# Low parts of the first slabs of a stage moved from GpSimd to VectorE, and let ahead of the norm

## The chip, the cores and the metric

The kernel runs on one core of a Trainium2 chip. The metric is the device time of one execution in microseconds (us), lower is better. Engines are named as in the profile: PE is TensorE (matmuls), DVE is VectorE, ACT is ScalarE, POOL is GpSimd, SP is the engine whose queue issues the weight loads.

## The reference

Two transformer blocks on 256 tokens of width 1024, all in float32. The first block has two layers (attention, then a convolution mixer), each followed by a squared-ReLU MLP and each with a layer norm after the residual; the second block has a retention and block-attention mixer and a retrieval over 16,384 experts.

```python
for l in range(2):                                   # first block
    sh1, sc1, g1, sh2, sc2, g2 = split(silu(c) @ ada_w[l] + ada_b[l], 6)      # conditioning
    h = x * (1 + sc1) + sh1
    y = even_mixer(h, ...) if l == 0 else conv_mixer(h, ...)                  # ends in  o @ w_out
    x = layer_norm(ALPHA * x + g1 * y, ln_g[l, 0], ln_b[l, 0])
    h = x * (1 + sc2) + sh2
    x = layer_norm(ALPHA * x + g2 * (square(relu(h @ mlp_w1[l])) @ mlp_w2[l]), ln_g[l, 1], ln_b[l, 1])
h = rmsnorm(x, mix_norm_g)                           # second block
rq, rk, rv, rg, mq, mk, mv, ga, gb = split(h @ w_in)
x = x + (sigmoid(ga) * y_a + sigmoid(gb) * y_b) @ w_out
x = x + peer(rmsnorm(x, ffn_norm_g), ...)
```

## The kernel before

Tokens lie in two tiles of 128. A large product is three matmuls: an operand is split into a high part (ACT copies it into the matmul's type) and a low part (the rest, one subtraction), and `mm3` (L117 to L119) adds high x high, high x low and low x high into one accumulator. Weights come in slabs of 256 rows x 512 columns: `slab` (L121) loads one (SP, 512 KB, into one of four `raw` buffers), makes its high part `whi` (ACT, L132) and its low part `wlo` (L133). A raw buffer is free for the next load when its low part is done. `whi` and `wlo` lie in a ring of five buffers each, freed by the matmuls that read them; the last slabs of a stage use a pool of their own.

A layer norm joins two stages. There are four such places in the program, called **joins** here:

- join 1, from about 223 to 255 us: attention's output projection, then the first MLP
- join 2, 430 to 468 us: the first MLP, then the convolution mixer
- join 3, 534 to 568 us: the convolution's output projection, then the second MLP
- join 4, 736 to 775 us: the second MLP, then the second block's mixer

At a join `add_norm` runs for token tile 0 and then tile 1. Per tile: two gated sums with the residual for each half of the columns (DVE, L409 from the accumulator, then L410), the mean `ln_m` (DVE, L413), the sum of squares (ACT, L416, called the Square below), a root on ACT (L171), four tiny DVE steps (L167, L172, L173 and L175), and the normed row (DVE, L422). Then `transpose_in` transposes it on PE (L195, eight transposes of 128 x 128), scales the pieces on DVE and ACT (`full`, L209 and L204) and splits them into `hT` (ACT L140, DVE L141). Those are the operand of the next stage's first slab group, which has 48 matmuls: four slabs, tile 0's 24 matmuls and then tile 1's 24 (`skew`).

Each engine works its list in order. The lists are laid down ahead of time by a scheduler; `issue_after` tells it to put one instruction behind another. Before the change the four slabs of a first slab group are `aside`: their high parts are placed behind tile 0's Square (`self.squared`), their low parts go to POOL. All other high parts wait to be placed behind tile 1's root (`self.rooted`), with low parts on DVE. Each slab also calls `tick`, which advances the background work: the conditioning of layer 1 (`ada_sums`), whose load, ACT or DVE multiply-add (L343, L346) and small matmuls are paced by it.

Of the kernel before, what the change touches and what calls it, by code (L numbers as in the profile page):

```python
# [9 lines left out]
F32 = mybir.dt.float32  # L10
# [4 lines left out]
AF = mybir.ActivationFunctionType  # L15
OP = mybir.AluOpType
# [5 lines left out]
KD = 8  # L22
# [61 lines left out]
class Net:  # L84
    def __init__(self, tc, ins, out, dbg):
        self.tc, self.nc, self.i, self.out, self.dbg = tc, tc.nc, ins, out, dbg
        self.bg = []
        self.n, self.pace, self.credit = 0, 1.2, 0.0
        self.squared = self.rooted = None
        self.mod, self.gate = {}, {}  # L90

    def name(self, p):
# [25 lines left out]
        nc.tensor.matmul(ps, ak(a[0]), bk(b[1]), start=False, stop=False, skip_group_check=True)  # L118
        self.last = nc.tensor.matmul(ps, ak(a[1]), bk(b[0]), start=False, stop=stop, skip_group_check=True)  # L119

    def slab(self, src, k0, c0, w=512, pool=None, aside=False):  # L121

        nc = self.nc
        self.tick()
        raw = self.raw.tile([128, 2, 512], F32, name="raw")
        nc.sync.dma_start(raw[:, :, :w], src[k0 * 128:(k0 + 2) * 128, c0:c0 + w].rearrange("(k p) n -> p k n", p=128))
        pool = pool or self.wsp
        hi = pool.tile([128, 2, 512], F32R, name="whi")
        lo = pool.tile([128, 2, 512], F32R, name="wlo")
        after = self.squared if aside else self.rooted  # L130
        with self.tc.issue_after(after.ins) if after else nullcontext():
            self.high = nc.scalar.activation(hi[:, :, :w], raw[:, :, :w], AF.Copy)  # L132
        low = (nc.gpsimd if aside else nc.vector).tensor_tensor(lo[:, :, :w], raw[:, :, :w],  # L133
                                                                hi[:, :, :w].bitcast(F32), op=OP.subtract)
        if not aside:
            self.low = low
        return hi, lo

    def split(self, full, hi, lo):
# [84 lines left out]
        return g  # L224


    def lin_T(self, src, c0, n, acts, k=KD, skew=(), last=None, aside=()):


        for c in range(0, n, 512):  # L230
            w = min(512, n - c)
            slabs = {}
            for p0 in range(0, len(acts), 2):
                pair = acts[p0:p0 + 2]
                ps = [self.acc() for _ in pair]
                for k0 in range(0, k, 2):
                    if k0 not in slabs:
                        slabs[k0] = self.slab(src, k0, c0 + c, w, last if c + 512 >= n else None, c // 512 in aside)
                order = [(k0, x) for k0 in range(0, k, 2) for x in range(len(pair))]
                if c // 512 in skew:  # L240
                    order.sort(key=lambda o: o[1])
                for k0, x in order:
                    h, t = pair[x]
                    s = slice(t * 128, (t + 1) * 128)
                    for m in range(2):
                        kk = k0 + m
                        self.mm3(ps[x][:, :w], h, slabs[k0], lambda a: a[:, kk, s], lambda b: b[:, m, :w],
                                 kk == 0, kk == k - 1)
                    if k0 + 2 == k:
                        yield (h, t), c // 512, ps[x]  # L250
# [15 lines left out]
    def lin_F(self, hT, src, c0, first=False):  # L266


        if first:
            for (h, t), c, ps in self.lin_T(src, c0, 512, [(hT, 0), (hT, 1)], skew=(0,), aside=(0,)):  # L270
                o = self.wd.tile([128, 512], F32, name="mr", bufs=2)
                self.nc.scalar.activation(o, ps, AF.Copy)
                p = self.wk()
                for n in range(4):
                    self.nc.tensor.transpose(p[:, n * 128:(n + 1) * 128], o[:, n * 128:(n + 1) * 128], self.ident)
                yield slice(0, 4), slice(t * 128, (t + 1) * 128), p.rearrange("p (n t) -> p n t", n=4)
            return
        ps = [self.wk() for _ in range(2)]
        for k0 in range(0, KD, 2):
            sl = self.slab(src, k0, c0)  # L280
            for n in range(4):
                for m in range(2):
                    kk = k0 + m
                    self.mm3(ps[n // 2][:, (n % 2) * 256:(n % 2 + 1) * 256], sl, hT,
                             lambda b: b[:, m, n * 128:(n + 1) * 128], lambda a: a[:, kk, :],
                             kk == 0 and n % 2 == 0, kk == KD - 1)
        for n in range(2):
            yield slice(2 * n, 2 * n + 2), slice(0, S), ps[n].rearrange("p (n t) -> p n t", n=2)
# [113 lines left out]
    def add_norm(self, t, ps, gate):  # L402

        nc = self.nc
        r = self.wd.tile([128, D], F32, name="resid", bufs=RES)
        sm = self.sm.tile([128, 2], F32, name="ln_s")
        for c in range(2):
            s = slice(c * 512, (c + 1) * 512)
            nc.vector.tensor_tensor(r[:, s], ps[c], gate[:, s], op=OP.mult)  # L409
            nc.vector.scalar_tensor_tensor(r[:, s], self.X[:, t, s], ALPHA, r[:, s], op0=OP.mult, op1=OP.add,  # L410
                                           accum_out=sm[:, c:c + 1])
        nm = self.sm.tile([128, 1], F32, name="ln_m")
        nc.vector.scalar_tensor_tensor(nm, sm[:, 0:1], sm[:, 1:2], self.rD, op0=OP.add, op1=OP.mult)  # L413
        j = self.wd.tile([128, D], BF16, name="junk", bufs=1)
        ss = self.sm.tile([128, 1], F32, name="ln_q")
        sq = nc.scalar.activation(j, r, AF.Square, bias=nm, accum_out=ss)  # L416
        if t == 0:
            self.squared = sq
        rs = self.rsqrt_of_sum(ss)
        if t == 1:  # L420
            self.rooted = self.root
        nc.vector.tensor_scalar(r, r, nm, rs, op0=OP.add, op1=OP.mult)  # L422
        return r
# [70 lines left out]
def rope_apply(net, z, nh, cosT, sinT, dst, halfview, rstd=None):  # L494

    nc = net.nc
    n = nh * 64
    t1 = net.wa.tile([128, 512], F32, name="rp1", bufs=1)
    t2 = net.wa.tile([128, 512], F32, name="rp2", bufs=1)
    z3 = z.rearrange("p (h d) -> p h d", h=nh)  # L500
    nc.vector.tensor_tensor(t1[:, :n].rearrange("p (h d) -> p h d", h=nh), z3,
                            cosT[:, None, :].to_broadcast([128, nh, 64]), op=OP.mult)
    a, w = halfview
    zv = z.rearrange("p (h a u w) -> p h a u w", h=nh, a=a, u=2)
    tv = t2[:, :n].rearrange("p (h a u w) -> p h a u w", h=nh, a=a, u=2)
    sv = sinT.rearrange("p (a u w) -> p a u w", a=a, u=2)
    for u in range(2):
        sb = sv[:, None, :, u, :].to_broadcast([128, nh, a, w])
        if a == 1:
            nc.vector.tensor_tensor(tv[:, :, 0, u, :], zv[:, :, 0, 1 - u, :], sb[:, :, 0, :], op=OP.mult)  # L510
        else:
            nc.vector.tensor_tensor(tv[:, :, :, u, :], zv[:, :, :, 1 - u, :], sb, op=OP.mult)
    if rstd is None:
        nc.vector.tensor_tensor(dst, t1[:, :n], t2[:, :n], op=OP.add)
    else:
        nc.vector.tensor_tensor(t1[:, :n], t1[:, :n], t2[:, :n], op=OP.add)
        nc.vector.tensor_tensor(dst.rearrange("p (h d) -> p h d", h=nh), t1[:, :n].rearrange("p (h d) -> p h d", h=nh),
                                rstd[:, :, None].to_broadcast([128, nh, 64]), op=OP.mult)
# [320 lines left out]
def second_mixer(net, hT, rs, done, ahead):  # L839
    nc, tc, i = net.nc, net.tc, net.i  # L840
    w = i["w_in_2"][0]
    act = [(hT, 0), (hT, 1)]
    with tc.tile_pool(name="m2", bufs=1, reuse_waits="tile") as mp:
# [3 lines left out]
        rv = net.x8([128, NT, D])  # L847
        gq = net.bcast(i["moba_q_gain_2"], 0, 64, "mgq", mp, 1)
        gk = net.bcast(i["moba_k_gain_2"], 0, 64, "mgk", mp, 1)
        nc.gpsimd.tensor_scalar(gq, gq, 0.125, 0.0, op0=OP.mult, op1=OP.add)  # L850
        for a in range(2):
            for (h, t), c, ps in net.lin_T(w, 512 * a, 512, act, skew=(0,) if a == 0 else (), aside=(0,) if a == 0 else ()):
                o = mp.tile([128, 512], F32, name="qk_o", bufs=2)
                dr = net.sm.tile([128, 8], F32, name="dr")
                nc.vector.tensor_scalar(dr, net.decay[:, t, a, :], rs[:, t:t + 1], None, op0=OP.mult)
                rope_apply(net, ps, 8, net.tabs[:, t, 2, :], net.tabs[:, t, 3, :], o, (1, 32), dr)
                trans4(net, o, qk[:, a, :, t * 128:(t + 1) * 128])
# [711 lines left out]
```

## Time and profile before

| | |
|---|---|
| time, median of 3 runs | 1904.43 us (1893.85 to 1904.66) |
| the profiled execution, its own time | 1892.69 us |
| its span in the profile | 1890.6 us |
| PE busy | 1804.4 us, 95% of the span |
| DVE busy | 1309.6 us, 69% |
| ACT busy | 864.3 us, 46% |
| POOL busy | 258.3 us, 14% |
| mean granted TensorE clock | 0.982 |
| chain of waits that ended last, by engine | PE 80%, DVE 14%, ACT 2%, DMA 2% |

The profile is one execution. Starts are counted from the start of the span, so a table of what one engine did in a stretch can be laid beside that of another. "Idle before" is what an engine waited just ahead of an instruction, with the instruction that ended it. Most of the program is limited by PE; the question for a change off PE is where PE stands still.

### The profile page before, as it was taken

What the parts mean: (1) busy time and instruction counts of PE and PEld (TensorE: products, weight loads), DVE (VectorE), ACT (ScalarE), POOL (GpSimd) and SP (SyncE); (2) the same over time, 40 slices, a digit from 0 to 9 for tenths busy, and PEclk for the clock granted to TensorE, in tenths of its full rate; (3) what the DMA queues carried; (4) which work ended last, traced back from release to release, by engine and by line L of the source; (5) the groups of instructions that cost most, each with busy time, mean ns of one, the idle gap of its engine ahead of it and who ended that gap; (6) DMA issues with size and microseconds to landing.
All of it is one profiled execution on the core that took longest, in us unless ns stands there. A gap on an engine that the chain in (4) does not pass through costs nothing.

```text
span 1890.6 us, 28661 instructions
## 1 busy us (share of the span) xinstructions
PE 1804.4 (95%) x10676; PEld 1513.8 (80%) x10676; DVE 1309.6 (69%) x3203; ACT 864.3 (46%) x1272; POOL 258.3 (14%) x182
## 2 busy tenths in 40 slices
PE   7999989997989997999999999999999999999998
PEld 4665679895978996775876499999999988888887
DVE  3665687768777555886576889979998145555554
ACT  2444555444445542545543244454444444444443
POOL 2000110002020002000000000045655810000000
PEclk9999999998999999898999999999999999999999
DMA  9755269886747564443666156644444666666664
GB/s 357 239 200 167 68 219 314 301 277 210 252 153 231 185 189 118 153 131 93 190 199 224 45 163 185 189 124 128 129 124 123 190 206 188 188 188 188 189 189 145
DMA packets 132155, 347.36 MB, mean 184 GB/s; under 512 B 12469, under 2 KB 13517, under 8 KB 130864
## 3 DMA queue, kind: packets, MB, share of 16 engines
q1 hardware_dynamic: 126752, 331.93, 55.0%
q0 software_dynamic: 4688, 12.03, 1.9%
q8 instruction: 84, 1.38, 0.3%
q10 hardware_dynamic: 576, 1.57, 0.2%
q14 instruction: 55, 0.45, 0.1%
HBM read 343.36 MB, written 3.70 MB: 184 GB/s over the span
## 4 chain that ended last, share of the span: by engine, by line
PE 80%; DVE 14%; DMA 2%; ACT 2%; issue 1%; SPq 0%; ACTq 0%; DVEq 0%
PE acc L117 19%; PE acc L119 19%; PE acc L118 19%; PE wk L117 4%; PE wk L118 4%; PE wk L119 4%; PE wk L1161 2%; DVE ulo L1187 2%; DVE x L1151 2%; PE wk L541 2%; PE acc L1023 1%; DVE ej L1111 1%; DVE x L1152 1%; DVE W L1174 1%; PE wk L375 1%
## 5 line engine op out<-in xcount | busy, mean ns | idle before, releaser
L1186 ACT ACTIVATE uhi<-raw 128x1024 fp32r<-128x1024 f32 x256 | 271.6, 1061 | 292.4 <-PE acc L119 177.8
L133 DVE TENSOR_TENSOR wlo<-raw,whi 128x1024 fp32r<-128x1024 f32 (+1 forms) x244 | 293.3, 1213 | 146.7 <-ACT whi L132 145.1
L132 ACT ACTIVATE whi<-raw 128x1024 fp32r<-128x1024 f32 (+1 forms) x260 | 270.5, 1051 | 258.6 <-PE acc L119 83.8
L1187 DVE TENSOR_TENSOR ulo<-raw,uhi 128x1024 fp32r<-128x1024 f32 x182 | 222.6, 1223 | 174.6 <-ACT uhi L1186 174.0
L117 PE MATMUL acc<-x,uhi 128*128 128x256 f32 x1024 | 293.8, 287 | 0.0
L118 PE MATMUL acc<-X,uhi 128*128 128x256 f32 x1024 | 288.6, 282 | 0.0
L119 PE MATMUL acc<-x,ulo 128*128 128x256 f32 x1024 | 288.4, 282 | 0.0
L117 PE MATMUL acc<-whi,hT 128*128 128x512 f32 (+1 forms) x528 | 212.8, 404 | 14.3 <-ACT hT L140 12.8
L1187 POOL TENSOR_TENSOR ulo<-raw,uhi 128x1024 fp32r<-128x1024 f32 x74 | 176.9, 2392 | 353.0 <-DVE x L1152 252.1
L118 PE MATMUL acc<-wlo,hT 128*128 128x512 f32 (+1 forms) x528 | 209.2, 396 | 1.0 <-DVE wlo L133 1.0
L119 PE MATMUL acc<-whi,hT 128*128 128x512 f32 (+1 forms) x528 | 208.4, 395 | 1.1 <-DVE hT L141 1.1
L117 PE MATMUL acc<-uhi,x 128*128 128x512 f32 x512 | 202.3, 395 | 1.0 <-ACT x L140 1.0
L119 PE MATMUL acc<-uhi,x 128*128 128x512 f32 x512 | 202.3, 395 | 0.0
L118 PE MATMUL acc<-ulo,x 128*128 128x512 f32 x512 | 202.2, 395 | 0.0
L117 PEld LDWEIGHTS acc<-x,uhi 128*128 128x128 f32 x1024 | 194.2, 190 | 0.2 <-issue 0.2
L118 PEld LDWEIGHTS acc<-X,uhi 128*128 128x128 f32 x1024 | 194.1, 190 | 0.2 <-issue 0.2
L119 PEld LDWEIGHTS acc<-x,ulo 128*128 128x128 f32 x1024 | 193.9, 189 | 0.0
L117 PE MATMUL wk<-hT,whi 128*128 128x256 f32 x608 | 172.6, 284 | 0.0
L118 PE MATMUL wk<-hT,whi 128*128 128x256 f32 x608 | 172.0, 283 | 0.0
L119 PE MATMUL wk<-hT,wlo 128*128 128x256 f32 x608 | 172.0, 283 | 0.0
L117 PEld LDWEIGHTS acc<-whi,hT 128*128 128x128 f32 x528 | 101.9, 193 | 47.0 <-ACT hT L140 15.9
L119 PEld LDWEIGHTS acc<-whi,hT 128*128 128x128 f32 x528 | 101.6, 192 | 27.4 <-issue 3.9
(359 smaller groups left out, 3145.8 us busy)
## 6 DMA issues: line engine op xcount, KB each, us to landing
raw<-in_mlp_w SPq DMA_DIRECT2D x128, 512.0 KB, 5.0
raw<-in_k_ut SPq DMA_DIRECT2D x128, 512.0 KB, 3.6
raw<-in_peer_v SPq DMA_DIRECT2D x128, 512.0 KB, 3.6
adaw<-in_ada_w SPq DMA_DIRECT2D x80, 512.0 KB, 4.9
raw<-in_w_in SPq DMA_DIRECT2D x52, 512.0 KB, 3.7
raw<-in_conv_w_in SPq DMA_DIRECT2D x24, 512.0 KB, 4.7
a<-in_k_a SPq DMA_DIRECT2D x8, 1024.0 KB, 9.3
raw<-in_attn_w_in SPq DMA_DIRECT2D x16, 512.0 KB, 8.6
```

The source lines that it names most:

```text
L117: nc.tensor.matmul(ps, ak(a[0]), bk(b[0]), start=start, stop=False, skip_group_check=True)
L118: nc.tensor.matmul(ps, ak(a[0]), bk(b[1]), start=False, stop=False, skip_group_check=True)
L119: self.last = nc.tensor.matmul(ps, ak(a[1]), bk(b[0]), start=False, stop=stop, skip_group_check=True)
L132: self.high = nc.scalar.activation(hi[:, :, :w], raw[:, :, :w], AF.Copy)
L133: low = (nc.gpsimd if aside else nc.vector).tensor_tensor(lo[:, :, :w], raw[:, :, :w], hi[:, :, :w].bitcast(F32), op=OP.subtract)
L375: nc.tensor.matmul(ps[32 * j:32 * j + 32, :], self.cT[:, k, :], raw[n - 1][:, m * 512:(m + 1) * 512], start=(k == 0), stop=(k == KD - 1), ...
L541: nc.tensor.transpose(p[:, k * 128:(k + 1) * 128], src[:, k * 128:(k + 1) * 128], net.ident)
L1023: nc.tensor.matmul(ps, self.hT[:, k, t * 128:(t + 1) * 128], self.slabs[c][k // 2][:, k % 2, j * n * 128:(j + 1) * n * 128], start=(k == 0 ...
L1151: nc.vector.tensor_scalar(a, self.places, col[:, 0, m:m + 1], col[:, 2, m:m + 1], op0=OP.is_equal, op1=OP.mult)
L1161: self.net.nc.tensor.matmul(self.p[:, k * 128:(k + 1) * 128], b, a, start=True, stop=True)
L1186: nc.scalar.activation(hi, raw, AF.Copy)
L1187: (nc.gpsimd if aside else nc.vector).tensor_tensor(lo, raw, hi.bitcast(F32), op=OP.subtract)
```

## The change

`aside` becomes `early`. The first slab group's low parts go to DVE like all the others; its high parts are no longer tied to tile 0's Square, nor to anything else, so the scheduler may put high and low parts ahead of the norm; and these slabs no longer call `tick`, so 4 background steps' worth of pace are left out at each of the four joins. Low parts on DVE are noted in `self.low` in every case, which the conditioning follows. A scale of a 64-wide vector (L850) goes from POOL to DVE with it.

```diff
-    def slab(self, src, k0, c0, w=512, pool=None, aside=False):
+    def slab(self, src, k0, c0, w=512, pool=None, early=False):
         nc = self.nc
-        self.tick()
+        if not early:
+            self.tick()
...
-        after = self.squared if aside else self.rooted
+        after = None if early else self.rooted
         with self.tc.issue_after(after.ins) if after else nullcontext():
             self.high = nc.scalar.activation(hi[:, :, :w], raw[:, :, :w], AF.Copy)
-        low = (nc.gpsimd if aside else nc.vector).tensor_tensor(lo[:, :, :w], raw[:, :, :w],
-                                                                hi[:, :, :w].bitcast(F32), op=OP.subtract)
-        if not aside:
-            self.low = low
+        self.low = nc.vector.tensor_tensor(lo[:, :, :w], raw[:, :, :w], hi[:, :, :w].bitcast(F32), op=OP.subtract)
...
-        sq = nc.scalar.activation(j, r, AF.Square, bias=nm, accum_out=ss)
-        if t == 0:
-            self.squared = sq
+        nc.scalar.activation(j, r, AF.Square, bias=nm, accum_out=ss)
...
-        nc.gpsimd.tensor_scalar(gq, gq, 0.125, 0.0, op0=OP.mult, op1=OP.add)
+        nc.vector.tensor_scalar(gq, gq, 0.125, None, op0=OP.mult)
```

How the lists move, at join 4. First DVE, from the last low parts of the second MLP to tile 0's normed row (the changed file's lines are two to four lower: L133 is L134 there, L409 L407, L422 L418). Before:

```order
L133 TENSOR_TENSOR wlo<-raw,whi 128x1024 x4
L409 TENSOR_TENSOR resid<-acc,gate 128x512
L410 SCALAR_TENSOR_TENSOR resid,ln_s<-X,resid 128x512
L409 TENSOR_TENSOR resid<-acc,gate 128x512
L410 SCALAR_TENSOR_TENSOR resid,ln_s<-X,resid 128x512
L413 SCALAR_TENSOR_TENSOR ln_m<-ln_s,rD 128x1
```

and of the change:

```order
L134 TENSOR_TENSOR wlo<-raw,whi 128x1024 x6
L407 TENSOR_TENSOR resid<-acc,gate 128x512
L134 TENSOR_TENSOR wlo<-raw,whi 128x1024
L408 SCALAR_TENSOR_TENSOR resid,ln_s<-X,resid 128x512
L407 TENSOR_TENSOR resid<-acc,gate 128x512
L134 TENSOR_TENSOR wlo<-raw,whi 128x1024
L408 SCALAR_TENSOR_TENSOR resid,ln_s<-X,resid 128x512
L407 TENSOR_TENSOR resid<-acc,gate 128x512
L411 SCALAR_TENSOR_TENSOR ln_m<-ln_s,rD 128x1
```

All four low parts of the first slab group now stand ahead of tile 0's mean. At joins 1 to 3 they are spread in the same way, at joins 1 and 2 all four ahead of the Square's result, at join 3 the last just ahead of the normed row.

Second, ACT at join 4, from the second MLP's last slabs to the root. Before:

```order
L132 ACTIVATE whi<-raw 128x1024 x4
L416 ACTIVATE junk,ln_q<-resid,ln_m 128x1024
L132 ACTIVATE whi<-raw 128x1024
L171 ACTIVATE rv_q<-ln_q,eps 128x1
L132 ACTIVATE whi<-raw 128x1024 x3
```

and of the change:

```order
L133 ACTIVATE whi<-raw 128x1024 x8
L414 ACTIVATE junk,ln_q<-resid,ln_m 128x1024
L169 ACTIVATE rv_q<-ln_q,eps 128x1
L414 ACTIVATE junk,ln_q<-resid,ln_m 128x1024
L202 ACTIVATE full<-wk,af3B,af3A 128x128 x2
```

All four high parts of the first slab group now stand ahead of tile 0's Square; so they do at joins 1 and 2, and two of them at join 3.

Third, PE at join 4, from the second MLP's last matmul. Before:

```order
L119 MATMUL acc<-whi,x_6571 128x512
L195 MATMUL wk<-ident,resid 128x128 x8
L117 MATMUL acc<-whi,hT 128x512
L118 MATMUL acc<-wlo,hT 128x512
L119 MATMUL acc<-whi,hT 128x512
L117 MATMUL acc<-whi,hT 128x512
L118 MATMUL acc<-wlo,hT 128x512
L195 MATMUL wk<-ident,resid 128x128 x8
```

and of the change:

```order
L119 MATMUL acc<-whi,x_6571 128x512
L193 MATMUL wk<-ident,resid 128x128 x16
L117 MATMUL acc<-whi,hT 128x512
L118 MATMUL acc<-wlo,hT 128x512
L119 MATMUL acc<-whi,hT 128x512
```

Tile 1's eight transposes now come ahead of every matmul of the first slab group; before, five of tile 0's matmuls stood between. At join 2 it is the same, with 15 matmuls between before. At joins 1 and 3 tile 0's transposes move the other way, 4 and 16 matmuls later into tile 1's share of the output projection (12 of its matmuls still followed at join 1 and now 8 do, 23 at join 3 and now 7).

## Rows read from the trace of the kernel before

**Rows 1.** Stretches: joins summed; first MLP (us, busy PE, PEld, DVE, ACT, POOL, PEclk).

```profile
sum 143.00, PE 102.22 PEld 79.86 DVE 108.96 ACT 63.61 POOL 46.01; mean PE 25.56 PEld 19.97 DVE 27.24 ACT 15.90 POOL 11.50
...
255.00:430.00 175.00, 174.31 (x1111) 157.43 (x1111) 136.54 (x138) 84.11 (x97) 5.77 (x12) 1.00 0.85 288
```

**Rows 2.** PE in order of time (start, us, what): transposes at the joins, two matmuls.

```profile
238.04 1.97 PE L195 MATMUL wk<-ident,resid 128*128 128x128 f32 x8 [5.26 <-DVE resid L422]
...
250.68 1.04 PE L195 MATMUL wk<-ident,resid 128*128 128x128 f32 x8
...
441.11 1.41 PE L195 MATMUL wk<-ident,resid 128*128 128x128 f32 x8 [4.26 <-DVE resid L422]
...
455.89 1.03 PE L195 MATMUL wk<-ident,resid 128*128 128x128 f32 x8
...
550.17 1.94 PE L195 MATMUL wk<-ident,resid 128*128 128x128 f32 x8 [6.06 <-DVE resid L422]
...
563.49 1.07 PE L195 MATMUL wk<-ident,resid 128*128 128x128 f32 x8 [0.17 <-DVE resid L422]
...
754.64 1.94 PE L195 MATMUL wk<-ident,resid 128*128 128x128 f32 x8 [9.70 <-DVE resid L422]
...
762.31 1.94 PE L195 MATMUL wk<-ident,resid 128*128 128x128 f32 x8 [0.16 <-DVE resid L422]
...
769.29 0.39 PE L117 MATMUL acc<-whi,hT 128*128 128x512 f32 x1
769.51 0.39 PE L118 MATMUL acc<-wlo,hT 128*128 128x512 f32 x1
```

**Rows 3.** DVE in order of time: the second-half sums, tile 0 (fourth: join 3's tile 1).

```profile
225.91 0.69 DVE L409 TENSOR_TENSOR resid<-acc,gate 128x512 f32<-128x512 f32 x1 [2.32 <-PE acc L119]
...
431.38 0.69 DVE L409 TENSOR_TENSOR resid<-acc,gate 128x512 f32<-128x512 f32 x1
...
538.44 0.69 DVE L409 TENSOR_TENSOR resid<-acc,gate 128x512 f32<-128x512 f32 x1 [2.76 <-PE acc L119]
...
558.57 0.69 DVE L409 TENSOR_TENSOR resid<-acc,gate 128x512 f32<-128x512 f32 x1 [2.21 <-PE acc L119]
...
739.48 0.69 DVE L409 TENSOR_TENSOR resid<-acc,gate 128x512 f32<-128x512 f32 x1 [1.32 <-PE acc L119]
```

**Rows 4.** DVE groups from 223 to 775 us: busy us, mean ns.

```profile
L133 DVE TENSOR_TENSOR wlo<-raw,whi 128x1024 fp32r<-128x1024 f32 x151 | 182.5, 1222 | 89.6 <-ACT whi L132 88.2 <-PE acc L119 0.8
...
L422 DVE TENSOR_SCALAR resid<-resid,ln_m,rv_o 128x1024 f32<-128x1024 f32 x8 | 15.9, 1984 | 0.2
L410 DVE SCALAR_TENSOR_TENSOR resid<-X,resid 128x512 f32<-128x512 f32 x15 | 15.7, 1047 | 0.3
...
L175 DVE SCALAR_TENSOR_TENSOR rv_o<-rv_z,rv_y 128x1 f32<-128x1 f32 x8 | 9.7, 1217 | 0.2
L173 DVE SCALAR_TENSOR_TENSOR rv_z<-rv_y,rv_v 128x1 f32<-128x1 f32 x8 | 8.9, 1108 | 0.2
```

**Rows 5.** The POOL group of low parts in the same stretch.

```profile
L133 POOL TENSOR_TENSOR wlo<-raw,whi 128x1024 fp32r<-128x1024 f32 x16 | 38.8, 2446 | 251.5 <-ACT whi L132 251.4
```

**Rows 6.** DVE in order of time at join 1, while POOL works on low parts.

```profile
230.70 1.63 DVE L173 SCALAR_TENSOR_TENSOR rv_z<-rv_y,rv_v 128x1 f32<-128x1 f32 x1
232.26 0.68 DVE L410 SCALAR_TENSOR_TENSOR resid<-X,resid 128x512 f32<-128x512 f32 x1
...
232.87 2.29 DVE L175 SCALAR_TENSOR_TENSOR rv_o<-rv_z,rv_y 128x1 f32<-128x1 f32 x1
```

**Rows 7.** Loads, KB each, median us to landing: joins 1, 2, 4, whole program.

```profile
raw<-in_mlp_w SPq DMA_DIRECT2D x4, 512.0 KB, 5.6
...
raw<-in_conv_w_in SPq DMA_DIRECT2D x4, 512.0 KB, 4.2
...
raw<-in_w_in SPq DMA_DIRECT2D x4, 512.0 KB, 3.5
...
raw<-in_attn_w_in SPq DMA_DIRECT2D x16, 512.0 KB, 8.6
```

More of the change, by code (lines that the diff above doesn't have):

```diff
@@ L88, in __init__ @@
         self.n, self.pace, self.credit = 0, 1.2, 0.0
-        self.squared = self.rooted = None
+        self.rooted = None
         self.mod, self.gate = {}, {}
@@ L224, in bcast, with lin_T @@
         return g
-    def lin_T(self, src, c0, n, acts, k=KD, skew=(), last=None, aside=()):
+    def lin_T(self, src, c0, n, acts, k=KD, skew=(), last=None, early=()):
         for c in range(0, n, 512):
@@ L237, in lin_T @@
                     if k0 not in slabs:
-                        slabs[k0] = self.slab(src, k0, c0 + c, w, last if c + 512 >= n else None, c // 512 in aside)
+                        slabs[k0] = self.slab(src, k0, c0 + c, w, last if c + 512 >= n else None, c // 512 in early)
                 order = [(k0, x) for k0 in range(0, k, 2) for x in range(len(pair))]
@@ L269, in lin_F @@
         if first:
-            for (h, t), c, ps in self.lin_T(src, c0, 512, [(hT, 0), (hT, 1)], skew=(0,), aside=(0,)):
+            for (h, t), c, ps in self.lin_T(src, c0, 512, [(hT, 0), (hT, 1)], skew=(0,), early=(0,)):
                 o = self.wd.tile([128, 512], F32, name="mr", bufs=2)
@@ L849, in second_mixer @@
         gk = net.bcast(i["moba_k_gain_2"], 0, 64, "mgk", mp, 1)
-        nc.gpsimd.tensor_scalar(gq, gq, 0.125, 0.0, op0=OP.mult, op1=OP.add)
+        nc.vector.tensor_scalar(gq, gq, 0.125, None, op0=OP.mult)
         for a in range(2):
-            for (h, t), c, ps in net.lin_T(w, 512 * a, 512, act, skew=(0,) if a == 0 else (), aside=(0,) if a == 0 else ()):
+            for (h, t), c, ps in net.lin_T(w, 512 * a, 512, act, skew=(0,) if a == 0 else (), early=(0,) if a == 0 else ()):
                 o = mp.tile([128, 512], F32, name="qk_o", bufs=2)
```

## The prediction

> **What bounds the kernel now.** I read the busy time by stretch first. The first MLP, between joins 1 and 2, keeps PE busy 174.31 of 175.00 us, so nothing off PE matters there; the four joins together last 143.0 us and hold 102.2 us of PE work, so PE stands still for 40.8 us in them [rows 1]. The change touches nothing else, and those 40.8 us, with the slow clock that follows a standstill, are all it can win.
>
> Next, PE in order of time at the joins [rows 2]. The longest waits are those of tile 0's transposes for the normed row on DVE: 5.26, 4.26, 6.06 and 9.70 us. How long should that norm take? Tile 1 of join 3 shows it undisturbed: its last sum starts at 558.57 when PE has finished the accumulator, and its transposes at 563.49, 4.92 us later [rows 2, 3]. Tile 0's last sums start at 225.91, 431.38, 538.44 and 739.48 [rows 3]; with 4.92 us their transposes would come at 230.8, 436.3, 543.4 and 744.4. They came at 238.04, 441.11, 550.17 and 754.64 [rows 2], later by 7.2, 4.8, 6.8 and 10.2, together 29.0 us.
>
> What stretches it shows in DVE's groups: over the joins the normed row takes 1984 ns in the mean, a half-width sum 1047, and two steps on a single column 1217 and 1108 [rows 4]. In order of time the latter took 1.63 and 2.29 us while POOL worked on low parts, and a half-width sum between them 0.68 [rows 6]. A POOL low part takes 2446 ns, and there are 16 in the joins, four at each [rows 5]: DVE's small steps wait out POOL's instruction in hand, one by one.
>
> **What is removed.** All 16 low parts leave POOL, and no other POOL arithmetic runs at the joins. I take the 29.0 us of delay as gone. The Trainium skill (GPSIMD Engine Reference, section 8, Key points) says that POOL shares its SBUF interfaces with VectorE and contends with its instructions in a two-port mode or with two SBUF inputs. By that rule the sum of 0.68 us, which has two SBUF inputs, would have been held too; the row says not all such instructions are, only those that meet a POOL instruction in hand. By the rule alone each join would have up to 2.45 - 0.68 = 1.8 us more to lose, 7 in all; I go by the starts above.
>
> **What is added on DVE.** Sixteen low parts of 1.22 us [rows 4], 4.9 a join, all ahead of tile 0's normed row. By the list tile 1's first half-width sums (0.69 + 0.68) come ahead of it too. Some of this lies in waits the norm has anyway (for the second accumulator, up to 2.76 us [rows 3], and for the Square). At joins 1 and 3 the second to fourth high parts need a ring buffer that tile 1's matmuls free one by one, 6 matmuls apart or 1.4 us at the pitch of 0.23 [rows 2], and at join 1 all stand before the Square. Walking down the lists with these durations I get tile 0's transposes 5.0, 5.1, 5.0 and 4.1 us behind the undisturbed times: at 235.8, 441.4, 548.4 and 748.5. The bounds for a join are 1.4 (every low part hidden) and 6.3 (none).
>
> **What each join gains.** Those starts are not the gain; PE's next wait is.
>
> Join 1. PE reaches the transposes 4 matmuls later than before, at 238.04 - 5.26 + 4 x 0.23 = 233.7, and waits 2.1 us. Transposes 1.04, eight output matmuls, and tile 1's last sum starts at 238.9; its norm takes 4.92 and finds two splits of tile 0 ahead on DVE (half-width too, so 0.7 each by the sums' row), so its transposes start at 245.2. Before: 250.68. Gain 5.5. This is at full clock. At the lower level (1.2 of 2.4 GHz; eight transposes took 1.94 against 1.04 [rows 2]) it is 0.9 and 8 x 0.2 less, 2.5.
>
> Join 3. PE has 16 more output matmuls ahead of the transposes, so it arrives at 550.17 - 6.06 + 16 x 0.23 = 547.8 and waits 0.6. Seven remain, tile 1's last sum starts at 551.0, its transposes at 551.0 + 4.92 + 1.4 = 557.4. Before: 563.49. Gain 6.1.
>
> Joins 2 and 4. All output matmuls are done, so PE stands still through both norms: tile 1's follows tile 0's on DVE 4.3 us behind, transposes at 445.7 and 752.9 (before: 455.89 and 762.31). What is given back: the matmuls of tile 0 that lay between, 15 and 5, now come after. PE's clock is at the lower level after such a standstill, and a matmul at half clock takes about 0.2 more. Join 2: before, from 455.89, transposes 1.0 and 33 matmuls x 0.23, end 464.5; now from 445.7, transposes 1.9, 48 x 0.23, nine of them at half clock 1.8, end 460.4: gain 4.1 (the small products that follow tile 1's transposes are in neither sum; they cost the same here or later). Join 4: before, 762.31 + 1.94 + 43 x 0.23, four at half clock 0.8, end 774.9; now 752.9 + 1.9 + 48 x 0.23, ten at half clock 2.0, end 767.8: gain 7.1.
>
> The conditioning steps that left the joins, loads, multiply-adds and products, run later beside PE-bound work, at no cost as long as the list ends them before the convolution's output projection, whose norm needs them; it does. Were DVE full there, PE would wait for a low part; in the first MLP it is busy 136.54 of 175.00 us [rows 1]. The 64-wide scale on DVE costs less than a half-width sum, and no DMA stands between its load and the join any more, so I put it at nothing.
>
> Sum: 5.5 + 4.1 + 6.1 + 7.1 = **22.8 us**, all on PE, and the stages behind are PE-bound, so it stays won. Against the profiled execution: 1892.69 - 22.8 = 1869.9. The median of the runs is 11.7 above that execution, and I forecast a median: 1904.43 - 22.8 = **1882**.
>
> **The rivals.**
>
> *The loads hold the norm.* At joins 1, 2 and 4 the fourth high part now stands ahead of tile 0's Square on ACT, and it needs its slab. I took loads of 5.6, 4.2 and 3.5 us; another weight takes 8.6 [rows 7]. At 8.6 each the Square would start 3.0, 4.4 and 5.1 us later, both tiles with it: the gain falls by 12.5 to 10.3, 1894. For: DVE and ACT keep strictly to their lists. Against: the raw buffers are freed by the previous stage's low parts, as before, and these loads were issued at those times already. Chance 0.30, for this and for gains half lost in other ways, as PE's clock staying low.
>
> *Slower: the norm waits for a late slab, and PE has lost its cover.* The same mechanism further on. At joins 2 and 4 tile 1's transposes now stand ahead of all 48 matmuls, so every us of a late slab is a us of PE. It decides when the fourth loads come more than 22.8 / 3 = 7.6 us later than I took, at 11 to 13 us. At 16 us: 10.4 + 11.8 + 12.5 = 34.7 lost, 12 net, 1916. Nothing at these joins comes near in the rows. Chance 0.05.
>
> *It does nothing.* The low parts cost the norm what POOL's contention cost it (6.3 a join against 29.0 / 4 = 7.2) and joins 1 and 3 hide behind output matmuls anyway. Then the gain is 4 x 0.9 = 4, 1900. Against: the walk above puts part of the low parts into waits. Chance 0.07.
>
> **How the numbers follow.** The forecast has 0.58. About 1% (19 us) is what a measurement of this kernel can tell from no change. The forecast's own spread (every low part hidden adds 3.6, 3.7, 3.6 and 2.7 to the gain, 36 at most; the clock staying low takes 2.5 at each of two joins, 17 at least) puts most of it beyond 19 us; the loads' rival falls within 1%. Faster 0.57, same 0.39, slower 0.04. The range: at the low end a gain of 27 on an execution like the profiled one, 1866; at the high end the loads' rival with a little more lost, 1897.
>
> **What would show it.** POOL's group of 16 low parts is gone and DVE's has 16 more; the normed row takes about 0.8 us in the mean, the one-column steps about 0.2. Tile 0's transposes wait about 2.1, 4.5, 0.6 and 4 us; at joins 2 and 4 PE waits again, some 2 to 3 us, for tile 1. PE's standstill over the four joins falls from 40.8 to about 23. I am wrong if DVE's sums or low parts are seen waiting for `whi`, if the Square starts behind a load, or if PE stands still in the MLPs.

## The result, and the profile after

| | before | after |
|---|---|---|
| median of the runs beside each other | 1902.63 us (4 runs) | 1866.67 us (4 runs) |
| ratio | | 0.985, 95% interval 0.981 to 0.989 |
| profiled execution, its own time | 1892.69 us | 1867.81 us |
| mean granted TensorE clock | 0.982 | 0.991 |

The change is faster by 1.5%. The profiled executions stand 24.9 us apart, where 22.8 were forecast. Executions of one kernel fall into two groups some 12 us apart (the 60 executions of before at 1889.97 to 1895.99 and at 1900.84 to 1907.46, almost half and half), so that a median jumps with the split, and "near group" below is the median of a kernel's faster group. It is 1892.8 for the kernel before and 1865.8 for the change (14 of its 16 executions), 27.0 apart.

The engines on the page of after (busy us, share of the span, instructions):

```profile
PE 1799.1 (96%) x10676; PEld 1508.8 (81%) x10676; DVE 1293.3 (69%) x3220; ACT 865.4 (46%) x1272; POOL 218.6 (12%) x165
```

The DVE groups of after from 223 to 775 us (busy, mean ns), which answer to [rows 4]:

```profile
L134 DVE TENSOR_TENSOR wlo<-raw,whi 128x1024 fp32r<-128x1024 f32 x180 | 216.8, 1221 | 91.1 <-ACT whi L133 90.4
L408 DVE SCALAR_TENSOR_TENSOR resid<-X,resid 128x512 f32<-128x512 f32 x15 | 10.3, 685 | 0.1
L418 DVE TENSOR_SCALAR resid<-resid,ln_m,rv_o 128x1024 f32<-128x1024 f32 x8 | 6.5, 811 | 0.2
L171 DVE SCALAR_TENSOR_TENSOR rv_z<-rv_y,rv_v 128x1 f32<-128x1 f32 x10 | 2.2, 216 | 0.2
L173 DVE SCALAR_TENSOR_TENSOR rv_o<-rv_z,rv_y 128x1 f32<-128x1 f32 x10 | 1.5, 154 | 0.2
```

Low parts are as long as before, 1221 ns. The normed row fell from 1984 to 811 ns, the two one-column steps from 1108 and 1217 to 216 and 154, the half-width sum from 1047 to 685. POOL's group of 16 low parts [rows 5] is gone. DVE has more to do and is busy 16.3 us less.

PE of after in order of time, the transposes that answer to [rows 2]:

```profile
238.00 1.09 PE L193 MATMUL wk<-ident,resid 128*128 128x128 f32 x8 [0.52 <-DVE resid L418]
...
247.01 1.03 PE L193 MATMUL wk<-ident,resid 128*128 128x128 f32 x8
...
437.51 1.86 PE L193 MATMUL wk<-ident,resid 128*128 128x128 f32 x8 [4.30 <-DVE up L818]
442.27 1.94 PE L193 MATMUL wk<-ident,resid 128*128 128x128 f32 x8 [2.90 <-DVE resid L418]
...
541.74 1.07 PE L193 MATMUL wk<-ident,resid 128*128 128x128 f32 x8
...
733.20 1.06 PE L193 MATMUL wk<-ident,resid 128*128 128x128 f32 x8 [2.72 <-DVE ln_m L411]
737.16 1.94 PE L193 MATMUL wk<-ident,resid 128*128 128x128 f32 x8 [2.90 <-DVE resid L418]
738.76 0.78 PE L117 MATMUL acc<-whi,hT 128*128 128x512 f32 x1
```

Tile 0 waits 0.52, 4.30, nothing and 2.72 us, against 5.26, 4.26, 6.06 and 9.70. ("DVE up" and "DVE ln_m" name the instruction that followed the normed row on DVE.) At joins 2 and 4 tile 1's transposes now wait 2.90 each.

The four joins as stretches, of before (which sum to [rows 1]) and then of after, chosen with about the same PE work (columns as in [rows 1]):

```profile
223.00:255.00 32.00, 24.11 (x100) 18.60 (x99) 23.07 (x36) 14.30 (x25) 10.87 (x5) 0.89 0.56 183
430.00:468.00 38.00, 26.16 (x116) 20.02 (x115) 33.16 (x53) 18.92 (x31) 11.61 (x7) 0.82 0.55 179
534.00:568.00 34.00, 25.88 (x112) 20.51 (x111) 21.74 (x38) 13.69 (x25) 10.33 (x5) 0.90 0.43 139
736.00:775.00 39.00, 26.08 (x106) 20.74 (x105) 31.00 (x47) 16.70 (x28) 13.20 (x11) 0.78 0.33 100
```

```profile
227.00:259.00 32.00, 28.23 (x132) 21.45 (x131) 25.66 (x47) 21.06 (x33) 1.58 (x3) 1.00 0.48 165
430.00:461.00 31.00, 23.11 (x89) 17.08 (x88) 22.93 (x47) 16.00 (x28) 2.19 (x3) 0.78 0.49 163
537.00:562.00 25.00, 21.92 (x102) 16.27 (x101) 20.71 (x38) 15.48 (x27) 1.41 (x3) 1.00 0.40 123
722.00:758.00 36.00, 30.38 (x134) 24.81 (x133) 30.84 (x67) 18.76 (x32) 2.12 (x4) 0.91 0.43 136
sum 124.00, PE 103.63 PEld 79.61 DVE 100.15 ACT 71.30 POOL 7.30; mean PE 25.91 PEld 19.90 DVE 25.04 ACT 17.83 POOL 1.82
```

PE stands still for 124.00 - 103.63 = 20.4 us instead of 40.8, and the granted clock no longer falls at joins 1 and 3 (1.00 in both, where it was 0.89 and 0.90). Over the whole span PE stands still 19.6 us less (66.6 after 86.2) and is busy 5.3 us less for the same 10,676 matmuls (1799.1 after 1804.4); together these are the 24.9 us between the two spans.

### The profile page after: what moved, and what is told of

Read it like the earlier page. It is cut to its first block, busy times and chain, and to the rows that moved or that the text cites. A ratio compares the mean times of both kernels' runs of the same rounds, so it can differ in the third digit from the quotient of the medians.

```text
span 1865.7 us, 28652 instructions
## 1 busy us (share of the span) xinstructions
PE 1799.1 (96%) x10676; PEld 1508.8 (81%) x10676; DVE 1293.3 (69%) x3220; ACT 865.4 (46%) x1272; POOL 218.6 (12%) x165
## 4 chain that ended last, share of the span: by engine, by line
PE 80%; DVE 13%; DMA 4%; ACT 2%; issue 1%; SPq 0%; ACTq 0%; DVEq 0%
PE acc L117 19%; PE acc L119 19%; PE acc L118 19%; PE wk L117 4%; PE wk L118 4%; PE wk L119 4%; DVE x L1147 2%; PE wk L1157 2%; DVE x L1148 2%; PE acc L1019 2%; PE wk L537 2%; DVE W L1170 1%; DVE ulo L1183 1%; PE wk L373 1%; DMA adaw<-in_ada_w 1%
## 5 line engine op out<-in xcount | busy, mean ns | idle before, releaser
L134 DVE TENSOR_TENSOR wlo<-raw,whi 128x1024 fp32r<-128x1024 f32 (+1 forms) x260 | 312.0, 1213 | 149.0 <-ACT whi L133 148.2
L133 ACT ACTIVATE whi<-raw 128x1024 fp32r<-128x1024 f32 (+1 forms) x260 | 270.5, 1051 | 271.5 <-PE acc L119 92.7
```

Of the source, the lines that this page charges most:

```text
L134: self.low = nc.vector.tensor_tensor(lo[:, :, :w], raw[:, :, :w], hi[:, :, :w].bitcast(F32), op=OP.subtract)
```

## The experiments

**Low parts alone on VectorE.** One edit to the kernel before:

```diff
-        low = (nc.gpsimd if aside else nc.vector).tensor_tensor(...)
+        low = nc.vector.tensor_tensor(...)
```

> The kernel before with one word changed: the 16 low parts of the joins are made on VectorE; their high parts stay behind tile 0's Square and the conditioning steps stay. After against before was 0.985, 28.5 us of 1902.6. Theory (GpSimd's low parts held the norm's small steps): most of the gain comes back, 18 to 28 us faster than before, ratio 0.985 to 0.991; one-column steps near 0.2 us. Rival 'order' (the slabs' freedom to come ahead of the norm made the gain): at most 8 us faster, 0.996 or more. Rival 'conditioning' (the steps that left the joins made it): also at most 8 us faster.

Ratio 0.988 (0.983 to 0.992), near group 1870.5: with the order as it was, the engine alone gives 22.3 of the 27.0 us, and 4.7 are left for the order and the steps. Its one-column steps took 219 and 159 ns. Both rivals fall. Tile 0's transposes waited at joins 2 and 4 only, 2.75 and 2.83 us.

**The other half: free order, low parts on GpSimd.**

```diff
-        self.low = nc.vector.tensor_tensor(lo[:, :, :w], ...)
+        low = (nc.gpsimd if early else nc.vector).tensor_tensor(lo[:, :, :w], ...)
+        if not early:
+            self.low = low
```

> The change with its 16 low parts of the joins back on GpSimd; high and low parts stay free to come ahead of the norm, no conditioning step with them. Theory: the contention is back, only partly ahead of the norm since the loads land around it, so 0 to 12 us faster than before, ratio 0.994 to 1.000; one-column steps of over 0.8 us in the mean. Rival 'order': 20 us faster or more, ratio 0.989 or less. Rival 'conditioning': the same 20 us or more.

Ratio 0.996 (0.993 to 0.999), near group 1882.0, 10.8 us gained; its twelve executions spread over 1878.74 to 1898.60 with the widest gap only 4.3 us, so this figure is the least certain of the near groups. The time is as the theory had it, but the detail missed: the one-column steps averaged 429 and 368 ns, not over 800, and the normed row 826. What was held there is what now coincided with GpSimd's work, the sums (1167 ns in the mean) and the mean of tile 0 (724 ns in the mean over both tiles, where it took 215 before). So the order is worth something while GpSimd makes the low parts: it moves part of that work away from the norm's last steps. VectorE at join 1, while GpSimd worked from 228.91 to 238.80:

```profile
230.44 1.43 DVE L410 SCALAR_TENSOR_TENSOR resid<-X,resid 128x512 f32<-128x512 f32 x1
...
231.91 2.23 DVE L413 SCALAR_TENSOR_TENSOR ln_m<-ln_s,rD 128x1 f32<-128x1 f32 x1
...
235.52 0.68 DVE L409 TENSOR_TENSOR resid<-acc,gate 128x512 f32<-128x512 f32 x1
...
236.67 2.67 DVE L410 SCALAR_TENSOR_TENSOR resid<-X,resid 128x512 f32<-128x512 f32 x1
```

**GpSimd work that nothing needs.** To the first experiment's kernel, for each slab of a first slab group:

```diff
+            h = hi[:, :, :w].bitcast(F32)
+            nc.gpsimd.tensor_tensor(raw[:, :, :w], h, h, op=OP.subtract)
```

> The run with the low parts on VectorE behind the Square, plus 16 subtractions on GpSimd that nothing needs: each takes the slab's high part twice and writes zeros over the slab's raw buffer once VectorE's low part has been made from it, so that VectorE's own list stays as it was and no matmul waits for GpSimd. The run without them took 1871 us at the median (0.988 of before). Theory (VectorE waits out GpSimd's instruction in hand): the gain goes, 15 to 35 us slower than that run, ratio to before 0.996 to 1.006, with one-column steps of over 0.8 us in the mean. Rival 'GpSimd's slower low part came late for the matmuls': the low parts are on VectorE here, so the time stays within 5 us of that run, ratio 0.985 to 0.991. Rival 'the raw buffers came free late, and the loads with them': these 16 hold their buffers 2.4 us longer again, 2 to 10 us slower, with one-column steps still near 0.2 us.

Ratio 1.000 (0.997 to 1.003), near group 1893.0: 22.5 us slower than without it, and the whole gain is gone. GpSimd's group from 223 to 775 us, and the held groups on VectorE:

```profile
L139 POOL TENSOR_TENSOR raw<-whi 128x1024 f32<-128x1024 f32 x16 | 35.8, 2243 | 271.3 <-DVE rv_z L176 189.1 <-DVE rv_y L175 68.1 <-DVE wlo L133 11.4
```

```profile
L425 DVE TENSOR_SCALAR resid<-resid,ln_m,rv_o 128x1024 f32<-128x1024 f32 x8 | 9.7, 1215 | 0.1
L178 DVE SCALAR_TENSOR_TENSOR rv_o<-rv_z,rv_y 128x1 f32<-128x1 f32 x8 | 5.8, 726 | 0.1
L176 DVE SCALAR_TENSOR_TENSOR rv_z<-rv_y,rv_v 128x1 f32<-128x1 f32 x8 | 5.6, 698 | 0.1
```

726 and 698 ns, a little under the 800 expected, and far from 200. No matmul waits for this work, so a late low part is no explanation. That the raw buffers were held longer cannot have stretched these rows, and it shows in no wait: from 215 to 790 us ScalarE waited 76.2 us for the MLP's slabs, against 74.9 in the run without the idle work, while PE's waits for the normed row and for `hT` grew from 19.8 to 38.4 us, 18.6 of the 20.3 us between the two profiled spans. Sixteen instructions on an engine at 14% of the span cost the kernel 22 us.

**The conditioning steps.** The change with each early slab's step back:

```diff
-        if not early:
-            self.tick()
+        self.tick()
```

> The change with the conditioning step of each early slab put back. Theory: the steps are loads, multiply-adds and small products that cost the same work anywhere; within 5 us of the change, ratio to before 0.983 to 0.988. Rival 'conditioning': 10 us or more of the gain is lost, ratio 0.990 or more.

Ratio 0.985 (0.982 to 0.988), all six executions at 1865.51 to 1870.68: within 2 us of the change. The steps cost nothing that shows at either place.

**The order alone.** The first experiment's kernel without those steps:

```diff
-        self.tick()
+        if not aside:
+            self.tick()
```

> The kernel before with the 16 low parts on VectorE and without the conditioning steps of these slabs; high parts stay behind tile 0's Square. It differs from the change by the order alone. Theory as forecast: the order is worth little either way, within 6 us of the change, ratio 0.982 to 0.989; the Square then doesn't wait for a late slab, which can make it faster than the change by up to 6. Rival 'order': slower than the change by 10 us or more, ratio 0.990 or more. Rival 'conditioning': like the change, while the run with the steps and low parts behind the Square is not.

Ratio 0.989 (0.985 to 0.993). Four of its six executions lie at 1880.10 to 1882.74 and two at 1866.82 and 1870.28. The profiled one is of the four, and what slows it lies past the joins (last section). This kernel differs from the change by a little more than the order: the 64-wide scale is still on GpSimd, and the early low parts are not noted in `self.low`; neither was tried alone. Against the change's profile this one took, from one join's end to the next, 2.1 us more at join 1, 2.0 less at join 2, 0.1 and 0.7 more at joins 3 and 4 (ends are PE's transposes of the first product, as shown below); three traces of the change itself differ by up to 2.4 at a join. In sum that is 0.9 us, and its two executions near the change's have a median of 1868.6, 2.8 us more: free order is worth some 3 us at most once the engine is right. The median alone, 14 us more, would have spoken for the rival 'order'.

**The change again, twice, as a control.**

> The change itself once more, as a control beside the next kernels: ratio 0.982 to 0.989 to before on every theory.

> The change itself as the control on the same chip: ratio 0.982 to 0.989 to before.

0.984 (0.981 to 0.987) and 0.983 (0.979 to 0.986).

**Late slabs.** In the change's trace ScalarE waits for slabs ahead of tile 0's Square (L414):

```profile
227.92 1.06 ACT L133 ACTIVATE whi<-raw 128x1024 fp32r<-128x1024 f32 x1 [3.42 <-DMA raw<-in_mlp_w]
...
234.31 1.15 ACT L414 ACTIVATE junk<-resid,ln_m 128x1024 bf16<-128x1024 f32 x1
...
430.19 1.06 ACT L133 ACTIVATE whi<-raw 128x1024 fp32r<-128x1024 f32 x1 [3.37 <-DMA raw<-in_conv_w_in]
432.68 1.15 ACT L414 ACTIVATE junk<-resid,ln_m 128x1024 bf16<-128x1024 f32 x1 [1.43 <-DVE ln_m L411]
```

```diff
-        after = None if early else self.rooted
+        after = (self.squared if k0 >= 4 else None) if early else self.rooted
...
```

(`self.squared` is set at tile 0's Square again, as before.)

> The change, with the third and fourth high part of each first slab group back behind tile 0's Square on ScalarE, so that no late slab can hold the Square. In the change's trace VectorE's low parts and ScalarE's high parts wait 3.4 us for a slab at join 1 and 3.4 at join 2, and the Square follows. Theory 'late slabs cost the norm': 2 to 6 us faster than the change, the Square at joins 1 and 2 starts within 1 us of the mean. Rival 'hidden at join 1 by the output projection, and given back as a wait for the high part': within 2 us of the change.

Ratio 0.985 (0.981 to 0.988), near group 1865.2, 0.6 us from the change (1.7 from the control on its chip, 1866.9). The rival holds: by itself the wait is worth nothing that can be told. At join 2 the third and fourth slab no longer stand ahead of the Square; at join 1 the longest wait, 3.32 us for the first slab, stays where it was. At join 2 tile 0's wait fell to 2.76 us and tile 1's rose to 3.85.

**The price of the low parts.** The change with the early low parts issued behind tile 0's normed row:

```diff
+        with self.tc.issue_after(self.normed.ins) if early else nullcontext():
             self.low = nc.vector.tensor_tensor(lo[:, :, :w], ...)
...
```

> The change, with the 16 low parts placed behind tile 0's normed row on VectorE; the high parts stay free. It prices the low parts in the norm's path, which the forecast took as 5.0, 5.1, 5.0 and 4.1 us less what waits hide. If they cost that at joins 2 and 4, where no output matmul hides it, tile 0's transposes come 3 us or more earlier against the last output matmul at each of the two, and the time falls by 3 to 8 us. Rival 'they lay in the wait for a slab anyway, and the low part comes late for the matmul instead': within 2 us of the change, with a wait for the low part in its place.

Neither. Tile 0's transposes came as early as expected (waits of 0.71 us at join 2 and none at join 4), and the time rose by 6.9 us (1872.7, ratio 0.987; 5.8 against the control on its chip). PE's waits from 223 to 775 us, of the change and then of this run:

```profile
PE wk L193 <- DVE resid L418: 6.3, 3, 2.9
PE wk L193 <- DVE up L818: 4.3, 1, 4.3
PE acc L117 <- ACT hT L138: 3.2, 4, 1.2
...
PE wk L193 <- DVE ln_m L411: 2.7, 1, 2.7
```

```profile
PE acc L117 <- ACT hT L139: 14.9, 6, 3.3
PE wk L194 <- DVE resid L419: 3.8, 4, 1.5
```

The wait moves from the transposes, 13.3 to 3.8, to the operand `hT`, 3.2 to 14.9: on VectorE's list the low parts now stand among the splits of tile 0 and the steps of tile 1's norm.

**The cover.** The change with tile 1's transposes at joins 2 and 4 traced inside the first slab group, behind the first 12 matmuls:

```diff
+                    if self.later and k0 == 4:
+                        turn, self.later = self.later, None
+                        with self.tc.issue_after(self.last.ins):
+                            turn()
...
```

(`turn` holds tile 1's `transpose_in`, which `self.later` puts off.)

> The change, with tile 1's eight transposes at joins 2 and 4 behind tile 0's first 12 matmuls instead of ahead of all 48. The forecast charged the change for the cover lost there: tile 1's transposes wait 2.90 and 2.90 us in its trace. If that cover is worth something, both waits go and the time falls by 2 to 6 us. Rival 'tile 0's operand is not split yet when tile 1's transposes come': the wait moves ahead of tile 0's first matmul and the time stays within 2 us of the change, or is up to 4 us longer as tile 1's operand comes later.

Ratio 0.987 (0.984 to 0.991), near group 1869.1, 3.3 slower (2.2 against the control on its chip). Both 2.90 waits went; the wait for `hT` grew to 8.4 us in all. By place: join 2 won 2.4 to 3.7 us against three traces of the change, join 4 lost 1.5 to 1.9.

**The two that looked best, together.** Two high parts behind the Square, and the cover at join 2 alone.

> The change with the two edits that looked best at their places: the third and fourth high part behind tile 0's Square, and at join 2 alone tile 1's transposes behind tile 0's first 12 matmuls. From the end of join 1's first slab group to that of join 2's the change took 202.5 and 201.2 us in two traces, the run with the cover kept 198.8. Theory 'these add up': 2 to 5 us faster than the change, some 1862 to 1865 us against a median of 1866.9. Rival 'the first slab group at a join ends on VectorE's work, whatever its order': within 2 us of the change.

Median 1861.99, ratio 0.981 (0.978 to 0.985), near group 1861.9 beside 1865.5 for the change on the same chip. Of these 3.6 us the two traces show 3.5 at join 2: from join 1's end to join 2's 199.0 us against 202.5 (201.2 to 202.5 in three traces of the change). It is clear of the kernel before; it leads the change by about 0.2%, with single executions of the two still overlapping (1859.31 to 1864.81 and 1861.96 to 1866.67), so that lead is not certain.

## Why the prediction was right

**What bounds.** Right. 40.8 us of standstill became 20.4 (about 23 forecast), and nothing else had to move but PE's own busy time, 5.3 us less.

**What is removed.** Right, and shown by two runs: taking the 16 low parts off POOL gives 22.3 us, giving POOL 16 idle instructions takes 22.5 back. From tile 0's last sums (230.16, 428.74, 532.42 and 725.78 in after's trace) to its transposes there are 7.8, 8.8, 9.3 and 7.4 us. Less 4.92 each, the norms are late by 2.9, 3.9, 4.4 and 2.5, together 13.7, where they were late by 29.0. Perhaps not all of the 29.0 was GpSimd's: in the run with the low parts behind the normed row, which has neither GpSimd's work nor a low part in the path, the starts (234.06, 433.49, 537.12 and 732.90, from sums at 226.59, 427.32, 530.72 and 727.34) are still late by 2.6, 1.3, 1.5 and 0.6, together 6 us. At joins 3 and 4 PE itself was not there earlier, so between 23 and 29 us went.

**The rule I set against one row.** I argued from the sum of 0.68 us [rows 6] that a sum with two SBUF inputs need not be held. It started only as the held step ahead of it ended; in the run with free order and low parts on GpSimd, sums of the same form that met a low part under way took 1.43 and 2.67 (above). So such a sum is held, and the sentence that I cited stands. The Trainium skill (SBUF — State Buffer, Who interferes with whom) says that the port pair that VectorE and GpSimd share is an exclusive lock, and that a VectorE instruction with two SBUF inputs contends with a GpSimd instruction that reads SBUF. The traces agree: a one-column step of 0.15 us took 2.29 beside a low part of 2.45.

**What is added.** Mis-sized, too high: 5.0, 5.1, 5.0 and 4.1 forecast, 2.9, 3.9, 4.4 and 2.5 measured, of which the run without them in the path lacks only 0.4, 2.6, 2.9 and 1.9. More of them fell into waits for PE's accumulators: VectorE's wait for these ahead of its sums fell from 12.0 to 2.1 us. Their place is not a loss: behind the norm they cost 6.9 us more.

**What each join gains.** The end of a join's first slab group shows as PE's transposes of its product. Before, and then after:

```profile
261.47 0.66 PE L275 MATMUL wk<-ident,mr 128*128 128x128 f32 x4 [0.69 <-ACT mr L272]
...
468.33 0.66 PE L275 MATMUL wk<-ident,mr 128*128 128x128 f32 x4 [0.69 <-ACT mr L272]
...
575.89 0.66 PE L275 MATMUL wk<-ident,mr 128*128 128x128 f32 x4 [0.46 <-ACT mr L272]
781.53 0.66 PE L541 MATMUL wk<-ident,qk_o 128*128 128x128 f32 x4
```

```profile
258.02 0.66 PE L273 MATMUL wk<-ident,mr 128*128 128x128 f32 x4 [0.46 <-ACT mr L270]
...
460.55 0.66 PE L273 MATMUL wk<-ident,mr 128*128 128x128 f32 x4 [0.69 <-ACT mr L270]
...
561.42 0.66 PE L273 MATMUL wk<-ident,mr 128*128 128x128 f32 x4 [0.46 <-ACT mr L270]
757.81 0.60 PE L537 MATMUL wk<-ident,qk_o 128*128 128x128 f32 x4
```

The spans between them shrank by 4.3, 6.7 and 9.3 us (206.86 to 202.53, 107.56 to 100.87, 205.64 to 196.39). Join 1, from tile 0's first sum on DVE (217.62 and 221.38), shrank by 7.2: this execution reached it 3.8 us later, in a part that the change does not touch (two other traces of the change reached it at 217.64 and 217.26). Over three traces of the change the four gains average 6.0, 4.8, 6.1 and 9.1, against 5.5, 4.1, 6.1 and 7.1. Join 4 is the term that was short. Tile 1's transposes were put 13.4 us behind tile 0's last sum (752.9 against 739.48) and came 11.4 behind it (737.16 against 725.78): the low parts added less, and tile 1 followed tile 0 by 4.0 us where 4.3 were taken. And of the ten matmuls that I let run at half clock, only the six from 738.76 on were slow, 0.8 us less.

**Against the median.** 1882 was 1904.43 - 22.8, but the median fell by 36.0 us, from 1902.63 to 1866.67, to the very edge of the range. The step that failed is "I forecast a median": the three times given (1893.85, 1904.43, 1904.66) had a gap of 10.6 us, and I should have forecast within one side of it and counted the other as a case. The forecast of 1882 was 15 us off for that reason. That the time still lies in the range is owed to its low end, which was worked out on the right side of the gap: a gain of 27 on an execution like the profiled one. The gain itself, 22.8, was a little small against the 24.9 and 27.0 that compare like with like.

**The rivals.** *The loads hold the norm*: the waits are there, and one of my signs of being wrong appeared with them: low parts waited for `whi` (1.67 us at join 1, 1.13 at join 2), with tile 0's mean and so the Square behind them. It cost little: taking the third and fourth slab out of the Square's way gained 0.6 us. *Slower*: the cover is lost, 2.90 us at each of two joins as forecast, but no slab came near the point from which it decides (the fourth load at join 2, which held the norm longest, took 5.9 us, and 11 to 13 were needed). *It does nothing*: refuted.

## What to carry to other kernels

An engine at 14% of the span can hold the critical path of another: look at the durations of tiny instructions (a one-column step of over 1 us) before the shares of busy time, and test by giving the suspected engine work that nothing needs. Once the contention was gone here, moving a step ahead or behind mostly moved the wait: of four such edits to the change two were slower, one was within 2 us, and the best gained 0.2%. Before forecasting a median, see whether the times given are of one group.

## What the runs showed of the hardware

Not every VectorE instruction is held by GpSimd. In the trace of before, GpSimd works on two low parts from 435.37 to 440.10:

```profile
435.50 0.16 DVE L172 RECIPROCAL rv_y<-rv_q 128x1 f32<-128x1 f32 x1
435.70 2.11 DVE L173 SCALAR_TENSOR_TENSOR rv_z<-rv_y,rv_v 128x1 f32<-128x1 f32 x1
437.85 2.27 DVE L175 SCALAR_TENSOR_TENSOR rv_o<-rv_z,rv_y 128x1 f32<-128x1 f32 x1
```

The reciprocal, with one input, runs in 0.16 us; the next two steps end as GpSimd's instructions do. A sum with its first input in the accumulator ran in 0.68 (L409 above, at 235.52). The number of inputs does not settle it alone: at join 3 of before the normed row, which reads one row from SBUF and two single columns, started while GpSimd was at work (542.48 to 552.24) and was held too, where it takes 0.81 us by itself:

```profile
547.23 2.79 DVE L422 TENSOR_SCALAR resid<-resid,ln_m,rv_o 128x1024 f32<-128x1024 f32 x1
```

The second surprise is a stretch of low clock far from the change. Stretches of 10 us from 835 us on, of the change and then of the order-alone run (the figure behind POOL's is the granted clock):

```profile
835.00:845.00 10.00, 6.71 (x26) 3.65 (x26) 6.34 (x21) 6.18 (x17) 1.48 (x3) 0.77 0.47 131
845.00:855.00 10.00, 10.00 (x45) 6.09 (x45) 5.29 (x21) 4.30 (x16) 1.33 (x3) 0.89 0.15 42
855.00:865.00 10.00, 10.00 (x47) 5.88 (x47) 6.14 (x22) 4.67 (x16) 0.00 (x0) 1.00 0.19 52
```

```profile
835.00:845.00 10.00, 7.85 (x22) 4.62 (x23) 5.86 (x20) 4.77 (x16) 1.45 (x3) 0.62 0.33 97
845.00:855.00 10.00, 10.00 (x30) 5.38 (x29) 3.09 (x12) 2.71 (x10) 0.54 (x1) 0.50 0.06 16
855.00:865.00 10.00, 10.00 (x27) 5.41 (x25) 2.71 (x12) 3.38 (x10) 0.54 (x1) 0.50 0.05 13
865.00:875.00 10.00, 10.00 (x27) 5.69 (x28) 3.90 (x13) 1.99 (x8) 0.00 (x0) 0.50 0.19 52
```

A PE wait of 3.29 us ends at 839.34 in the change and at 837.15 in the other, and behind it the granted clock is at 1.2 of 2.4 GHz in both. In the change it is back within some 10 us; in the other it stays down past 875 while PE is busy throughout, with 27 to 30 matmuls in 10 us instead of 45 to 47. From the first to the last of the same 24 small products (`sme`, which start at that wait) the change took 29.8 us and the other 46.2: these 16.4 us are more than the 13.7 by which its span is longer, so what slows that execution is this stretch. Whether other executions that took some 12 us more have the same cause was not seen, since the other profiled ones are not of that kind. Why the clock stayed down here stays open.
